# Attention scores as pairs of 64-row matmuls, with later transposes in the recurrence and a third plain MLP tile

## The chip, the core and the metric

The kernel runs on one core of a Trainium2 chip. Its engines work from queues of their own, each in order: TensorE (PE; loads of weights are shown apart as PEld), VectorE (DVE), ScalarE (ACT), GpSimd (POOL) and SyncE (SP), which here issues the DMAs. TensorE multiplies a moving operand (up to 512 columns) by weights that lie in its array of 128 rows and 128 columns, and writes to PSUM, eight banks of 512 f32 columns. The metric is the device time of one execution in microseconds.

## The reference

One layer of a diffusion backbone, batch 1, 1024 latent tokens with 256 context tokens ahead, width 1024, f32. What matters here:

```python
# inside each layer
aq, ak, av, bq, bk, bv, cq, cf, cb, ci, cg, gates = features(h_lat, w_in, ...)   # h @ w_in, split; rope, RMS of heads
yc = hgrn2_bidir(cq, cf, cb, ci, cg, ...)            # recurrence in both directions, 4 heads of 128
ya = window_attn(aq, ak, av, cak, cav, sink_a)       # 8 heads of 64, 2 kv heads; 256 context keys + band of 3 blocks + sink
yb = global_attn(bq, bk, bv, cbk, cbv)               # 8 heads of 64, 2 kv heads; 256 context + 1024 latent keys
x_mix = x + m_lat[2] * (sum_n sigmoid(gate_n) * (y_n @ w_branch[n])) @ w_out
u = dwconv(h2 @ w_up, w_dw, b_dw)                    # two halves a and g of 2816 channels, conv over 3 tokens
x = x_mix + m_lat[5] * ((a * silu(g)) @ w_down)
out = rms_norm(x, norm_final)
```

The scores are `q . k / 8`, in the attention of both kinds with 4 query heads per kv head; the softmax is over all keys that a query may see. In the recurrence the output of each head is RMS-normed over its 128 channels, scaled and multiplied by `silu(cg)`.

## The kernel before

f32 products are made from two parts. A value is split into a high part that TensorE's f32r format holds and the rest (`h` and `l`, written by an ACT copy and a DVE subtraction); a product of matrices is three f32r matmuls, high by high, high by low, low by high (L199 to L201, L841 to L843, L917 to L919).

The stages follow each other: modulation and context, the recurrence head by head (`hgrn_head`, L1040), token-major projections with rope, window attention, global attention, merging of the branches, output projection, the MLP's up products, its down products, the last norm.

**Attention.** Each of 16 iterations takes 128 queries and one kv head, so 4 query heads. `qprep` splits the queries and lays, for each head, 64 rows of high part and 64 rows of low part one above the other, so that QT[:, h] has 128 rows. The keys stand twice in KH and twice in KL, in rows 0 to 63 and again in rows 64 to 127. One matmul of QT[:, h] with KH gives (high + low) by high, one with KL (high + low) by low: two matmuls per head and group of keys give all four products of parts. `softmax_window` (L1351) makes the scores of one head in one two-bank PSUM tile (tag mm, two of them: L1364 and L1365 for the context, L1367 and L1368 for the band, L1369 adds the mask), and DVE takes the maximum, ACT the exponential with the sum. `softmax_global` (L1392) makes the context scores of four heads in one tile (L1402, L1403) and then, head by head, 1024 latent scores in a tile each (L1412, L1413). The probabilities are transposed (L1298), split (L1302 and L1303) and multiplied with the values (L1284, L1285). Products for the merge gates (L199 to L201, tile gz) serve as filler. `weave` interleaves the scores of the next iteration, the values of this one and the filler by step counts; the framework's scheduler then sets each engine's order from data dependencies, priorities and its own estimates of duration.

**Recurrence.** `hgrn_head` ends, for each half of the tokens, with 12 matmuls for the output tile o (L1164 to L1166), ACT's square (L1167), DVE's sum, POOL's power, DVE's scaling into yo (L1172), four transposes oT of yo (L1175), DVE's product with gain and gate (L1177) and a store. The next head's projections (zf, zb) follow in the program and may be drawn ahead by the scheduler.

**MLP, up.** Of 22 tiles of 128 channels in each half, tiles 0 and 1 are plain products (`plain`, L755). From tile 2 on a recursive scheme with seven block products instead of eight is used (`w_sums`, `up_first`, `up_rest`), which needs sums of the weights and of the blocks of the activations: T1, T2, T3 and T4, made by DVE and ACT after tile 1. T4 takes the place of the block named 12. `act_out` does the convolution and the gate, `act_store` the store. L867 is DVE's sum that frees half of a PSUM tile in `up_rest`.

Of the kernel before, what the change touches and what calls it, by code (L numbers as in the profile page):

```python
# [18 lines left out]
P = 128  # L19
# [48 lines left out]
NB = 1  # L68
# [23 lines left out]
def build(tc, ins, out, dbg=None):  # L92
    nc = tc.nc
    V, A, G, T, SP = nc.vector, nc.scalar, nc.gpsimd, nc.tensor, nc.sync
    with ExitStack() as top:
# [697 lines left out]
        act_out(1, za)  # L793

        blk["T4"] = blk["12"]
# [4 lines left out]
        P1[0] = Aligned(p1s.enter_context(tc.tile_pool(name="p1", bufs=1, side="right", reuse_waits="tile")))  # L800

# [238 lines left out]
def hgrn_head(nc, cp, h, proj, early, mm2, bank, ident, masks, lb, oml, st_ctx, gnc, mhalf, y_d):  # L1040
# [116 lines left out]
    for g in range(2):  # L1157
        yo = cp.tile([P, 4, P], F32, tag="yo", name=f"yo{h}{g}", bufs=2)
        ys = cp.tile([P, 512], F32, tag="ys", name=f"ys{h}{g}", bufs=2)
        pt = bank("b", f"o{h}{g}")  # L1160
# [6 lines left out]
        A.activation(yo, pt, AF.Square)  # L1167
        rs = cp.tile([P, 4], F32, tag="ors", name=f"ors{h}{g}", bufs=2)
        V.reduce_sum(out=rs, in_=yo, axis=AX.X)
        V.tensor_scalar(out=rs, in0=rs, scalar1=1.0 / P, scalar2=EPS, op0=ALU.mult, op1=ALU.add)  # L1170
        G.tensor_tensor(out=rs, in0=rs, in1=mhalf[:, :4], op=ALU.pow)
        V.tensor_tensor(out=yo, in0=pt, in1=rs[:, :, None].to_broadcast([P, 4, P]), op=ALU.mult)  # L1172
        pt2 = bank("b", f"oT{h}{g}")
        for c in range(4):
            T.transpose(pt2[:, c], yo[:, c], ident)  # L1175
        sl = slice(g * 512, g * 512 + 512)
        V.scalar_tensor_tensor(out=ys, in0=pt2.rearrange("p a b -> p (a b)"), scalar=gnc, in1=cg[:, sl],  # L1177
                               op0=ALU.mult, op1=ALU.mult)
        SP.dma_start(y_d[2, h][:, sl], ys)
# [26 lines left out]
def attention(tc, nc, ap_, br, ins, kv_d, q_d, y_d, mm2, bank, ident, identr, fill_gen, fill_steps):  # L1206
# [45 lines left out]
    def qprep(it):  # L1252
# [4 lines left out]
        qs = tl([P, 4, 2, 64], "qs", f"q{it}", dt=F32R)  # L1257
        A.activation(qs[:, :, 0], qf, AF.Copy, scale=QSCALE)
        V.scalar_tensor_tensor(out=qs[:, :, 1], in0=qf, scalar=QSCALE, in1=qs[:, :, 0].bitcast(F32),
                               op0=ALU.mult, op1=ALU.subtract)  # L1260
# [79 lines left out]
    for it in range(n_it):  # L1340
# [4 lines left out]
        weave((scores(it + 1), S_LEN * (4 + br)) if it + 1 < n_it else (None, 0),  # L1345
              (values(it, PT, kts), len(kts) + 1),
              (some(fill_gen, b - a), b - a))
    man.close()


def softmax_window(nc, tl, mm2, tt, g, nm, QT, KH, KL, trir, identr, snk, nsnk, res):  # L1351
# [9 lines left out]
    for h in range(4):  # L1361

        sc = mm2(f"sa{nm}{h}").rearrange("p a b -> p (a b)")[:, 256:256 + nk]
        T.matmul(sc[:, :256], QT[:, h], KH[:, g, :256], start=True, stop=False)  # L1364
        T.matmul(sc[:, :256], QT[:, h], KL[:, g, :256], start=False, stop=True)  # L1365
        k = (2 + lo) * P
        T.matmul(sc[:, 256:], QT[:, h], KH[:, g, k:k + w], start=True, stop=False)  # L1367
        T.matmul(sc[:, 256:], QT[:, h], KL[:, g, k:k + w], start=False, stop=False)  # L1368
        T.matmul(sc[:, 256:], identr, trir[:, m0:m0 + w], start=False, stop=True)  # L1369
        n1 = ng[:, h:h + 1]  # L1370
        hs = g * 4 + h
        V.tensor_reduce(out=n1, in_=sc, axis=AX.X, op=ALU.max, negate=True)

        V.tensor_tensor(out=n1, in0=n1, in1=nsnk[:, hs:hs + 1], op=ALU.min)
        pw = tl([P, 640], "pw", f"{nm}{h}", 8)
        A.activation(pw[:, :nk], sc, AF.Exp, bias=n1, accum_out=sm[:, h:h + 1])
        Ps.append(pw)
        if h % NB == NB - 1:
            b = slice(h - NB + 1, h + 1)
            bs = slice(hs - NB + 1, hs + 1)  # L1380
# [4 lines left out]
            for j in range(h - NB + 1, h + 1):  # L1385
                G.tensor_scalar(out=Ps[j][:, :nk], in0=Ps[j][:, :nk], scalar1=sm[:, j:j + 1], scalar2=1.0,
                                op0=ALU.mult, op1=ALU.mult)
# [4 lines left out]
def softmax_global(nc, tl, mm2, g, nm, QT, KH, KL, res, rs):  # L1392
# [5 lines left out]
    nc_, ng, sm, r = st[:, 0], st[:, 1], st[:, 2:4], st[:, 4]  # L1398
    pc = tl([P, 4, 256], "pc", nm)
    sc = mm2(f"sbc{nm}").rearrange("p a (b c) -> p (a b) c", b=2)  # L1400
    for h in range(4):
        T.matmul(sc[:, h], QT[:, h], KH[:, g, :256], start=True, stop=False)  # L1402
        T.matmul(sc[:, h], QT[:, h], KL[:, g, :256], start=False, stop=True)  # L1403
# [4 lines left out]
    for h in range(4):  # L1408
        s2 = mm2(f"sbl{nm}{h}")
        for hf in range(2):  # L1410
            k = 256 + hf * 512
# [142 lines left out]
```

## Time and profile before

| | |
|---|---|
| median of 3 runs | 2142.07 us (2141.16 to 2144.56) |
| the profiled execution's own time | 2145.39 us |
| its span | 2143.6 us |
| TensorE busy | 2089.5 us, 97% of the span |
| DVE, ACT, POOL busy | 1391.7, 1005.2, 301.0 us |
| recurrence, heads 0 to 3 | about 159 to 445 us |
| window attention scores | from 708.1 us to 885.9 us |
| global attention | from about 918 us to 1228 us |
| recursive up tiles | from about 1490 us to 1881 us |

A row of the groups or of the timeline names a line, an engine, the operation, what it writes and reads, the array's rows and columns used (128\*64: 128 rows, 64 columns), the shape, and the time. In the timeline the first number is the start and the second how long the instruction or the merged group took; a matmul's end is modelled, and neighbours overlap, so the distance between starts says how long one holds the engine. A bracket is idle time before the instruction, with the one that ended it. In the busy times by stage the columns are the stretch, its length, the busy time and count of PE, PEld, DVE, ACT and POOL, the granted PE clock, and two of DMA.

### The profile page before, as it was taken

How to read it: one execution, taken by the hardware profiler on the slowest of the kernel's cores; microseconds unless marked ns; L12 is line 12 of the kernel's file. 1: busy time of each engine (PE TensorE's matmuls, PEld its weight loads, DVE VectorE, ACT ScalarE, POOL GpSimd, SP SyncE). 2: the span in 40 equal slices, each digit the busy share in tenths (PEclk: the TensorE clock that was granted, in tenths of full speed). 3: DMA queues.
4: the chain of work that ended last, by engine and by line, in shares of the span. 5: the costliest groups of instructions: out<-in, count | busy, mean ns of one | idle time of the engine just before them, and what ended most of it. 6: DMA issues, size and time to landing. Idle time of an engine off the chain costs nothing. (4 is left out here: it accounts for less than half of the span.)

```text
span 2143.6 us, 30557 instructions
## 1 busy us (share of the span) xinstructions
PE 2089.5 (97%) x11674; PEld 1741.4 (81%) x11674; DVE 1391.7 (65%) x2306; ACT 1005.2 (47%) x1768; POOL 301.0 (14%) x262
## 2 busy tenths in 40 slices
PE   7999999999999999999999999999999999999997
PEld 4887887888988888878888788887788888888887
DVE  4736746626565687678887746569777777664433
ACT  3333322411122777688888734346445444453322
POOL 0001000010022222100000000011533444200111
PEclk9999999999999999999999999999999999999999
DMA  9511111126644221211100354541222222285342
GB/s 352 210 43 41 39 41 40 50 97 206 198 136 130 77 60 41 73 66 35 35 28 28 115 197 145 191 158 40 98 89 80 78 89 79 89 289 193 107 127 89
DMA packets 95492, 229.29 MB, mean 107 GB/s; under 512 B 10737, under 2 KB 35825, under 8 KB 94321
## 3 DMA queue, kind: packets, MB, share of 16 engines
q1 hardware_dynamic: 95344, 227.33, 32.0%
q8 instruction: 92, 1.51, 0.3%
q14 instruction: 56, 0.45, 0.1%
HBM read 181.68 MB, written 45.61 MB: 106 GB/s over the span
## 5 line engine op out<-in xcount | busy, mean ns | idle before, releaser
L175 ACT CAST wh<-wr 128x1024 fp32r<-128x1024 f32 x137 | 143.3, 1046 | 401.2 <-PE dn L918 73.2
L176 DVE TENSOR_TENSOR wl<-wr,wh 128x1024 fp32r<-128x1024 f32 x137 | 168.9, 1233 | 240.6 <-ACT wh L175 227.2
L1303 DVE TENSOR_TENSOR pl<-pp,ph 128x512 fp32r<-128x512 f32 x236 | 159.5, 688 | 29.1 <-ACT ph L1302 23.3
L199 PE MATMUL gz<-hh,wh 128*128 128x512 f32 x384 | 156.2, 407 | 3.6 <-ACT gs L523 3.5
L1302 ACT CAST ph<-pp 128x512 fp32r<-128x512 f32 x236 | 135.7, 587 | 37.5 <-PE pp L1298 35.4
L201 PE MATMUL gz<-hh,wl 128*128 128x512 f32 x384 | 152.2, 397 | 0.0
L200 PE MATMUL gz<-hl,wh 128*128 128x512 f32 x384 | 152.2, 396 | 0.0
L210 PE MATMUL tm<-wl,hh 128*128 128x256 f32 x384 | 108.9, 283 | 3.1 <-DVE wl L176 3.1
L209 PE MATMUL tm<-wh,hh 128*128 128x256 f32 x384 | 108.8, 283 | 0.7 <-ACT qo L613 0.7
L211 PE MATMUL tm<-wh,hl 128*128 128x256 f32 x384 | 108.6, 283 | 0.0
L1284 PE MATMUL po<-ph,VHL 128*128 128x512 f32 x236 | 106.1, 450 | 1.5 <-ACT ph L1302 1.0
L918 PE MATMUL dn<-ac,wh 128*128 128x512 f32 x256 | 99.7, 390 | 0.0
L919 PE MATMUL dn<-ac,wl 128*128 128x512 f32 x256 | 99.6, 389 | 0.0
L917 PE MATMUL dn<-ac,wh 128*128 128x512 f32 x256 | 99.6, 390 | 0.0
L1285 PE MATMUL po<-pl,VHL 128*128 128x512 f32 x236 | 97.0, 411 | 0.1
L199 PEld LDWEIGHTS gz<-hh,wh 128*128 128x128 f32 x384 | 72.8, 189 | 17.7 <-ACT gs L523 5.7
L201 PEld LDWEIGHTS gz<-hh,wl 128*128 128x128 f32 x384 | 72.5, 189 | 14.9
L200 PEld LDWEIGHTS gz<-hl,wh 128*128 128x128 f32 x384 | 72.8, 190 | 11.6
L731 ACT ACTIVATE u<-c,cw 128x1024 f32<-128x1024 f32 x40 | 50.0, 1249 | 66.3 <-DVE c L878 35.5
L210 PEld LDWEIGHTS tm<-wl,hh 128*128 128x128 f32 x384 | 73.7, 192 | 4.1 <-DVE wl L176 3.7
L1298 PE MATMUL pp<-ident,plat 128*128 128x128 f32 x512 | 76.7, 273 | 0.0
L1298 PEld LDWEIGHTS pp<-ident,plat 128*128 128x128 f32 x512 | 62.8, 140 | 16.9 <-DVE pl L1303 1.2
(1448 smaller groups left out, 5958.8 us busy)
## 6 DMA issues: line engine op xcount, KB each, us to landing
wr<-in_w_cm SPq DMA_DIRECT2D x48, 512.0 KB, 3.6
wr<-in_w_up SPq DMA_DIRECT2D x44, 512.0 KB, 3.5
wr<-in_w_down SPq DMA_DIRECT2D x33, 512.0 KB, 3.5
wmr<-in_w_mod SPq DMA_DIRECT2D x32, 512.0 KB, 4.6
gate_d<-gs SPq DMA_DIRECT2D x48, 256.0 KB, 2.4
sgt<-gate_d SPq DMA_DIRECT2D x24, 512.0 KB, 3.4
act_d<-u SPq DMA_DIRECT2D x22, 512.0 KB, 2.6
st<-act_d SPq DMA_DIRECT2D x44, 256.0 KB, 3.8
```

The lines of the kernel that those rows point to most:

```text
L175: A.copy(hi[:, :n], raw[:, :n])
L176: (lo_eng or V).tensor_tensor(out=lo[:, :n], in0=raw[:, :n], in1=hi[:, :n].bitcast(F32), op=ALU.subtract)
L199: T.matmul(psl, wh[:, k, c], hh[:, k0 + k, cols], start=s, stop=False)
L200: T.matmul(psl, wh[:, k, c], hl[:, k0 + k, cols], start=False, stop=False)
L201: T.matmul(psl, wl[:, k, c], hh[:, k0 + k, cols], start=False, stop=e)
L209: T.matmul(psl, hh[:, k, toks], wh[:, k % 4, :], start=s, stop=False)
L210: T.matmul(psl, hh[:, k, toks], wl[:, k % 4, :], start=False, stop=False)
L211: T.matmul(psl, hl[:, k, toks], wh[:, k % 4, :], start=False, stop=e)
L1284: T.matmul(po, vv, ph, start=n == 0, stop=False)
L1298: T.transpose(pp[:, h], PT(h, n), ident)
L1302: A.copy(ph, pp)
L1303: V.tensor_tensor(out=pl, in0=pp, in1=ph.bitcast(F32), op=ALU.subtract)
```

## The change

Three edits.

*Scores.* `qprep` now lays the high parts of two heads one above the other, and their low parts likewise, so that rows 0 to 63 hold one head and rows 64 to 127 another. Each score group is made by `pair_scores`: three products (high by high, low by high, high by low; low by low is left out) for the two heads in turn, each a matmul over 64 rows of the array, head 2a in rows 0 to 63 and head 2a + 1 in rows 64 to 127, in different PSUM tiles. A pair takes both tiles of tag mm. The context scores in the global stage lie in another order of heads. QT has two buffers instead of three, and the step counts of `weave` change (2 + br in place of 4 + br).

*Recurrence.* The norm up to yo stays where it was, and the transposes with what follows them become a function (`turn`) that the next head calls behind its two forget gates; for the last head the gate products that follow call them.

*MLP.* Tile 2 of the up products is a plain one; its second-half products of the first four blocks stand ahead of T4's split, the rest behind it.

```diff
-            for h in range(CH):
-                hgrn_head(nc, c1, h, proj, early, mm2, bank, ident, masks, lb, oml, st_ctx, gnc, mhalf, y_d)
+            late = []
+            for h in range(CH):
+                late = hgrn_head(nc, c1, h, proj, early, mm2, bank, ident, masks, lb, oml, st_ctx, gnc, mhalf, y_d, late)
             for n, i in gates[:4]:
-                for _ in gate_unit(c1, n, i, "mm"):
-                    pass
+                for j, _ in enumerate(gate_unit(c1, n, i, "mm")):
+                    if late and j % 8 == 7:
+                        late.pop(0)()
...
+        ws = up_units(2)
+        za = [mm2(f"up2{s}") for s in (1, 0)][::-1]
+
+        for s in (1, 0):
+            plain([za[s][:, 1]], [ws[s]], 1, range(KQ))
         blk["T4"] = blk["12"]
...
+        for s in (1, 0):
+            plain([za[s][:, 1]], [ws[s]], 1, range(KQ, KT))
+            plain([za[s][:, 0]], [ws[s]], 0, range(KT))
+        act_store()
+        act_out(2, [[z.rearrange("p a b -> p (a b)")] for z in za])
...
-        for f in range(2, FT):
+        for f in range(3, FT):
...
         forget(nc, cp, z, F1[:, d], KS[:, d], lb[:, d * 4 + h:d * 4 + h + 1], oml[:, d * 4 + h:d * 4 + h + 1],
                L, f"{nm}{h}")
+        if late:
+            late.pop(0)()
...
+        def turn():
+            pt2 = bank("b", f"oT{h}{g}")
+            for c in range(4):
+                T.transpose(pt2[:, c], yo[:, c], ident)
...
+        return turn
...
-        for h in range(4):
-            T.transpose(pq[:, h], qs[:, h].rearrange("p a b -> p (a b)"), identr)
-        QT = tl([P, 4, P], "QT", it, 3, F32R)
+        for part in range(2):
+            for a in range(2):
+                T.transpose(pq[:, 2 * part + a], qs[:, part, 2 * a:2 * a + 2].rearrange("p a b -> p (a b)"), identr)
+        QT = tl([P, 4, P], "QT", it, 2, F32R)
...
-        weave((scores(it + 1), S_LEN * (4 + br)) if it + 1 < n_it else (None, 0),
+        weave((scores(it + 1), S_LEN * (2 + br)) if it + 1 < n_it else (None, 0),
...
+def pair_scores(T, zs, a, QT, KH, KL, g, k, n, more=False):
+
+    for j, (part, K) in enumerate(((0, KH), (1, KH), (0, KL))):
+        for r, z in enumerate(zs):
+            rows = slice(r * 64, r * 64 + 64)
+            T.matmul(z, QT[rows, 2 * part + a], K[rows, g, k:k + n], start=j == 0, stop=j == 2 and not more)
...
-        T.matmul(sc[:, :256], QT[:, h], KH[:, g, :256], start=True, stop=False)
-        T.matmul(sc[:, :256], QT[:, h], KL[:, g, :256], start=False, stop=True)
...
+        scs = [mm2(f"sa{nm}{2 * a + r}").rearrange("p a b -> p (a b)")[:, 256:256 + nk] for r in range(2)]
+        pair_scores(T, [sc[:, :256] for sc in scs], a, QT, KH, KL, g, 0, 256)
+        pair_scores(T, [sc[:, 256:] for sc in scs], a, QT, KH, KL, g, (2 + lo) * P, w, True)
...
-    for h in range(4):
-        s2 = mm2(f"sbl{nm}{h}")
+    for a in range(2):
+        s2 = [mm2(f"sbl{nm}{2 * a + r}") for r in range(2)]
         for hf in range(2):
-            k = 256 + hf * 512
-            T.matmul(s2[:, hf], QT[:, h], KH[:, g, k:k + 512], start=True, stop=False)
-            T.matmul(s2[:, hf], QT[:, h], KL[:, g, k:k + 512], start=False, stop=True)
+            pair_scores(T, [s_[:, hf] for s_ in s2], a, QT, KH, KL, g, 256 + hf * 512, 512)
```

How the order of the instructions moves is seen at three places of TensorE's queue. First the global stage, the third and fourth head of iteration 4 (tiles sbl_2 and sbl_3). Before, the two matmuls of each 512 keys stand together, one head at a time:

```order
4441 L200 MATMUL gz_9659<-hl,wh_9655 128x512
4442 L201 MATMUL gz_9659<-hh,wl_9656 128x512
4443 L1412 MATMUL sbl_2_9736<-KH_0_8659,QT_4_9414 128x512
4444 L1413 MATMUL sbl_2_9736<-KL_0_8660,QT_4_9414 128x512
4445 L1412 MATMUL sbl_2_9736<-KH_0_8659,QT_4_9414 128x512
4446 L1413 MATMUL sbl_2_9736<-KL_0_8660,QT_4_9414 128x512
4447 L1298 MATMUL pp_9746<-ident,plat_3_0_9458 128x128
```

Now (x2 stands for two such matmuls in a row):

```order
4556 L1321 MATMUL pp_9959<-ident,plat_3_3_9719 128x128
4557 L1379 MATMUL sbl_2_9931<-KH_0_8787,QT_4_9578 128x512 x2
4558 L1379 MATMUL sbl_2_9931<-KL_0_8788,QT_4_9578 128x512
4559 L1379 MATMUL sbl_2_9931<-KH_0_8787,QT_4_9578 128x512 x2
4560 L1379 MATMUL sbl_2_9931<-KL_0_8788,QT_4_9578 128x512
4561 L1307 MATMUL po_9823<-ph_34_9911,VHL_0_8789 128x512
4562 L1379 MATMUL sbl_3_9932<-KH_0_8787,QT_4_9578 128x512 x2
4563 L1379 MATMUL sbl_3_9932<-KL_0_8788,QT_4_9578 128x512
4564 L1379 MATMUL sbl_3_9932<-KH_0_8787,QT_4_9578 128x512 x2
4565 L1379 MATMUL sbl_3_9932<-KL_0_8788,QT_4_9578 128x512
```

The two heads were written in turn, matmul by matmul; in the queue all six of the one head stand ahead of all six of the other.

Second the window stage, the first heads of iteration 6 (tiles sa_0 and sa_1). Before, one head's five matmuls:

```order
3282 L1364 MATMUL sa_0_7072<-KH_0_5968,QT_6_6914 128x256
3283 L1365 MATMUL sa_0_7072<-KL_0_5969,QT_6_6914 128x256
3284 L1367 MATMUL sa_0_7072<-KH_0_5968,QT_6_6914 128x384
3285 L1368 MATMUL sa_0_7072<-KL_0_5969,QT_6_6914 128x384
3286 L1369 MATMUL sa_0_7072<-trir_0_5973,identr 128x384
```

Now:

```order
3312 L1286 MATMUL pq_7112<-identr,qs_q_7109 128x128
3313 L1379 MATMUL sa_0_7120<-KH_0_5968,QT_6_6954 128x256
3314 L1379 MATMUL sa_1_7121<-KH_0_5968,QT_6_6954 128x256
3315 L1379 MATMUL sa_0_7120<-KH_0_5968,QT_6_6954 128x256
3316 L1379 MATMUL sa_1_7121<-KH_0_5968,QT_6_6954 128x256
3317 L1379 MATMUL sa_0_7120<-KL_0_5969,QT_6_6954 128x256
3318 L1379 MATMUL sa_1_7121<-KL_0_5969,QT_6_6954 128x256
```

Here the heads alternate in the queue as they do in the program.

Third the recurrence, the outputs o and transposes oT of head 0. Before, the transposes of the first half stand ahead of the outputs of the second:

```order
414 L201 MATMUL zf_1515<-hh,wl_1512 128x512
...
416 L200 MATMUL zf_1515<-hl,wh_1511 128x512
417 L1175 MATMUL oT_1413<-ident,yo_1392 128x128 x4
418 L1164 MATMUL o_1422<-Vt_1046,S_1117 128x128
419 L1165 MATMUL o_1422<-ST_1331,QQ_986 128x128
```

Now:

```order
416 L1198 MATMUL o_1413<-ST_1331,QQ_986 128x128
417 L1199 MATMUL o_1413<-ST_1331,QQ_986 128x128
418 L198 MATMUL zf_1501<-hh,wh_1497 128x512
...
429 L200 MATMUL zf_1501<-hh,wl_1498 128x512
430 L1183 MATMUL oT_1555<-ident,yo_1405 128x128 x4
431 L198 MATMUL zb_1568<-hh,wh_1564 128x512
```

The outputs of both halves come first, then twelve products of the next head's zf, then the first transposes.

More of the change, by code (lines that the diff above doesn't have):

```diff
@@ L1037, in head_rms, with hgrn_head @@
     return r
[L1040 removed]
+def hgrn_head(nc, cp, h, proj, early, mm2, bank, ident, masks, lb, oml, st_ctx, gnc, mhalf, y_d, late):
     V, A, G, T, SP = nc.vector, nc.scalar, nc.gpsimd, nc.tensor, nc.sync
@@ L1166, in hgrn_head @@
             T.matmul(o, QQ[:, 0, sl], ST[:, 1, c], start=False, stop=True)
[L1167 to L1179, printed above, removed]
+        late.append(norm(g, pt))
+    return late
 def some(gen, n):
@@ L1384, in softmax_window @@
             V.reciprocal(sm[:, b], sm[:, b])
-            for j in range(h - NB + 1, h + 1):
-                G.tensor_scalar(out=Ps[j][:, :nk], in0=Ps[j][:, :nk], scalar1=sm[:, j:j + 1], scalar2=1.0,
-                                op0=ALU.mult, op1=ALU.mult)
+            G.tensor_scalar(out=pw[:, :nk], in0=pw[:, :nk], scalar1=sm[:, b], scalar2=1.0, op0=ALU.mult, op1=ALU.mult)
         yield
@@ L1397, in softmax_global @@
     st = tl([P, 5, 4], "st", nm)
-    nc_, ng, sm, r = st[:, 0], st[:, 1], st[:, 2:4], st[:, 4]
+    nc_, ng, sm = st[:, 0], st[:, 1], st[:, 2:4]
     pc = tl([P, 4, 256], "pc", nm)
[L1400 to L1403, printed above, removed]
+    sc = mm2(f"sbc{nm}").rearrange("p r (a c) -> p r a c", a=2)
+    for a in range(2):
+        pair_scores(T, [sc[:, r, a] for r in range(2)], a, QT, KH, KL, g, 0, 256)
+    sc = sc.rearrange("p r a c -> p (r a) c")
     V.tensor_reduce(out=nc_, in_=sc, axis=AX.X, op=ALU.max, negate=True)
```

73 lines of the change are left out of this document (42 added, 31 removed).

## The prediction

> **What bounds the kernel now.** I read the page first, then the busy time by stage, then the waits of TensorE, then single starts in its timeline. The page says that TensorE (PE) has work nearly all the time; the two attention stages, where the scores are made, say it more sharply:
>
> ```profile
> span 2143.6 us, 30557 instructions
> PE 2089.5 (97%) x11674; PEld 1741.4 (81%) x11674; DVE 1391.7 (65%) x2306; ACT 1005.2 (47%) x1768; POOL 301.0 (14%) x262
> ...
> 720.00:890.00 170.00, 169.11 (x1009) 145.85 (x1008) 134.82 (x414) 124.28 (x320) 47.44 (x61) 1.00 0.16 50
> 935.00:1210.00 275.00, 273.47 (x1587) 224.76 (x1586) 222.48 (x373) 226.40 (x487) 6.04 (x15) 1.00 0.10 32
> ```
>
> In the window stage (720 to 890 us) PE is busy 99%, in the global stage (935 to 1210) 99%, at the full granted clock, while DVE and ACT stand at 80% and 82%. The score matmuls hardly wait for another engine: this group has the most, 1.3 us in 128 matmuls, for what ACT had still to read from a scores buffer.
>
> ```profile
> L1412 PE MATMUL sbl<-KH,QT 128*128 128x512 f32 x128 | 51.8, 405 | 1.3 <-ACT pc__8872 L1405 1.3
> ```
>
> So attention takes as long as its matmuls take to issue one behind another. "Busy" does not price that, since neighbours overlap; the distance between starts does.
>
> ```profile
> 1502.06 0.39 PE L842 MATMUL upd<-T1l,ws2h 128*128 128x512 f32 x1
> 1502.29 0.39 PE L843 MATMUL upd<-T1h,ws2l 128*128 128x512 f32 x1
> 1502.52 0.39 PE L841 MATMUL upd<-T1h,ws2h 128*128 128x512 f32 x1
> ...
> 2117.82 0.33 PE L917 MATMUL dl<-ac,wh 128*128 128x384 f32 x1
> 2118.86 0.33 PE L917 MATMUL dl<-ac,wh 128*128 128x384 f32 x1
> ...
> 1076.25 0.60 PE L1298 MATMUL pp<-ident,plat 128*128 128x128 f32 x4
> 1076.61 0.47 PE L1284 MATMUL po<-ph,VHL 128*128 128x512 f32 x1
> 1076.92 0.39 PE L1285 MATMUL po<-pl,VHL 128*128 128x512 f32 x1
> 1077.18 0.50 PE L1284 MATMUL po<-ph,VHL 128*128 128x512 f32 x1
> 1077.52 0.28 PE L1402 MATMUL sbc__10700<-KH,QT 128*128 128x256 f32 x1
> 1077.63 0.28 PE L1403 MATMUL sbc__10700<-KL,QT 128*128 128x256 f32 x1
> 1077.75 0.28 PE L1402 MATMUL sbc__10700<-KH,QT 128*128 128x256 f32 x1
> ...
> 2127.10 0.28 PE L917 MATMUL dl<-ac,wh 128*128 128x128 f32 x1
> 2127.21 0.28 PE L918 MATMUL dl<-ac,wh 128*128 128x128 f32 x1
> ```
>
> A slot of 512 columns costs 0.227 us, one of 384 costs 0.174 (2117.82 to 2118.86 in six steps), one of 256 costs 0.12. The 128-column pair stops at 0.11, above a quarter of 0.227: a load of 128 columns of weights takes that long, and is hidden under every wider matmul. After a transpose (1076.61 to 1076.92) the first plain matmul holds PE 0.31, 0.086 more.
>
> **The scores, slot by slot.** Before: per head two matmuls over all 128 rows. The loops give 288 slots of 256 columns (160 window, 128 global), 96 of 384 and 256 of 512: 288 x 0.12 + 96 x 0.174 + 256 x 0.227 = 109.4 us. After: 432, 144 and 384 matmuls of 64 rows each, half as many again, which pay only where one on rows 0-63 and one on rows 64-127 run at once, so where they are neighbours in PE's order. The trace has no 64-row matmul. It has pairs side by side in 64 columns each, the recurrence's scores:
>
> ```profile
> 168.06 0.39 PE L201 MATMUL zq<-hh,wl 128*128 128x512 f32 x1
> 168.28 0.39 PE L199 MATMUL zq<-hh,wh 128*128 128x512 f32 x1
> 168.60 1.15 PE L1106 MATMUL sc<-QQ,KC 128*64 128x64 f32 x32
> 169.68 0.50 PE L200 MATMUL zq<-hl,wh 128*128 128x512 f32 x1
> 170.02 0.39 PE L201 MATMUL zq<-hh,wl 128*128 128x512 f32 x1
> 170.25 0.40 PE L199 MATMUL zq<-hh,wh 128*128 128x512 f32 x1
> ...
> L1106 PE MATMUL sc<-QQ,KC x768: 222/222/272, 159.9 to 420.1; 128*64 128x64 f32 x192
> ...
> 200.63 0.39 PE L1164 MATMUL o<-Vt,S 128*128 128x128 f32 x2
> 200.85 0.39 PE L1165 MATMUL o<-ST,QQ 128*128 128x128 f32 x2
> ```
>
> An f32 matmul is recorded as two passes. The 32 passes of L1106 start within 1.15 - 0.22 = 0.93 us, 0.030 each. An undivided f32 pass over 128 columns takes 0.11 (two in 0.22, L1164 to L1165), so one over 64 would take 0.055: the pairs do overlap, and their weight loads with them. I take the same for rows.
>
> But the order decides what overlaps. In the global stage the second pair of heads stands as six matmuls of head 2, one value product, six of head 3: both need an emptied buffer, and the scheduler started each when its own was free. All six are on one half of the rows. Counted over PE's whole order, a matmul sharing a slot only with a neighbour on the other half, the changed kernel needs 260 slots of 256, 84 of 384 and 315 of 512: 31.2 + 14.6 + 71.5 = 117.3 us. That is **7.9 us more** than before; the window stage wins 3.1 of it (35.9 to 32.8), the global stage loses 11 (73.5 to 84.5).
>
> **The switch between shapes.** The same rows price it. L199 at 168.28 holds PE 0.32 before the divided array may start, 0.09 over its slot. Behind it (last pass starts 1.15 - 0.22 after 168.60, at 169.53) the next whole-array matmul starts 0.15 later where 0.05 would do: 0.10. Then L200 holds PE 0.34, 0.11 over its slot: its successor's weights could not be loaded ahead. Is that a matter of columns alone? A 2-row transpose, rows divided and columns whole, shows the way out too:
>
> ```profile
> 39.71 0.28 PE L305 MATMUL pm<-ident,row 2*128 2x2 f32 x2 [0.30 <-ACT row L349]
> 39.92 3.72 PE L432 MATMUL czf<-ch,wr 128*128 128x256 f32 x16
> 43.48 2.75 PE L432 MATMUL czb<-ch,wh 128*128 128x256 f32 x12
> ```
>
> The twelve take 2.75 - 0.38 = 11 x 0.216; the sixteen behind the switch take 3.34, 0.10 more than 15 x 0.216. So rows cost the same. The Trainium skill says this too: TensorEngine Tiling (Array Packing), section Key Properties, has it that changing the tiling mode, not just the tile, drains the engine. It speaks against this change: by it the free switch below falls away for 64 rows too, where the rows above, none of them with 64 rows, leave it open.
>
> In the changed order the 64-row matmuls stand in 150 stretches (38 window, 112 global), cut by transposes, value products and gate products. Way in: 0.09 plus one exposed load of 0.11, 0.20 each: 30 us. Way out: 89 times to a plain matmul, 0.10 + 0.11; 61 times to a transpose, whose load is half as long, 0.10 + 0.055: 28 us. In return 41 of the 313 transpose-to-matmul steps go, at 0.086: -3.5. Switches: **+54.5 us**. Bounds: nothing, if rows switch free; and, if the loads of the two halves do not overlap, 0.11 more on each way in (16), 0.10 on each of the 172 shared 256-slots (17) and 0.05 on the 60 shared 384-slots (3), so +36. I take 54.5, since its parts come from the nearest shapes.
>
> A pair now holds both scores buffers. The order puts some 26 PE rows, about 5 us, between a pair and the next, and a slower PE leaves ACT and DVE more time: 0, at most 0.3 us for each of 32 pairs (10 us).
>
> **The later transposes.** PE stands before the output transposes of each head:
>
> ```profile
> L1175 PE MATMUL oT<-ident,yo 128*128 128x128 f32 x32 | 5.2, 284 | 7.1 <-DVE yo L1172 7.1
> ...
> 200.14 0.66 PE L1175 MATMUL oT<-ident,yo 128*128 128x128 f32 x4 [0.98 <-DVE yo L1172]
> ```
>
> Eight waits, 7.1 us. In the new order twelve products of the next head, 12 x 0.227 = 2.7 us, stand behind the second half's outputs and ahead of the first transposes, so that wait goes in three heads. The last head has no next one: its transposes follow directly and keep their two waits. Gain 7.1 x 6/8 = **5.3 us** (0 to 7.1).
>
> **The third plain tile.** 96 matmuls instead of 84: 12 x 0.227 = 2.7 us more. It takes PE past a place where DVE is behind with the split blocks:
>
> ```profile
> 1498.08 0.50 PE L843 MATMUL upc<-T3h,vlS 128*128 128x512 f32 x1 [0.33 <-DVE vlS L680]
> ...
> 1505.47 0.50 PE L841 MATMUL up<-T2h,ws2h 128*128 128x512 f32 x1 [2.12 <-DVE c L867]
> ...
> 1527.71 0.66 PE L841 MATMUL up<-T2h,ws3h 128*128 128x512 f32 x1 [2.90 <-DVE c L867]
> 1528.17 0.63 PE L842 MATMUL up<-T2l,ws3h 128*128 128x512 f32 x1
> 1528.60 0.63 PE L843 MATMUL up<-T2h,ws3l 128*128 128x512 f32 x1
> ...
> 1528.00:1532.00 4.00, 4.00 (x12) 3.09 (x12) 1.00 (x1) 0.00 (x0) 3.92 (x4) 0.59 0.03 6
> ```
>
> Three waits, 5.35 us, and behind the longest the granted clock falls to 0.59: eight matmuls at 0.427 instead of 0.227, 1.6 us. With 96 x 0.227 = 21.8 us of products that need little of DVE, it catches up. Net 2.7 - 5.35 - 1.6 = **-4.3 us** (up to +2.7 if the waits only move on to the next tile's sum, L867).
>
> **Sum.** 7.9 + 54.5 - 5.3 - 4.3 = +52.8 us, on the profiled execution's 2145.4: 2198. That execution stood 3.3 over the median of 2142.1, so 2195.
>
> **Rivals.** *The switch is free for rows* (not slower): one mechanism, PE keeping its queue filled across shapes, at the 300 borders of the stretches. 7.9, plus 1.7 for 20 more transpose-to-matmul steps, minus 9.6: 0, so 2142. It decides from a border cost of nothing; each 0.01 us puts 3 us on it. For it: a 64-row tile keeps all 128 columns. Against it: the 2-row rows. Faster by much would take neighbours everywhere, 109.4 x 3/4 (27 less, 2105), which the order rules out.
> *Half price*: only the drains, or only the loads: 2168.
> *Weight loads do not hide*: the two halves load in turn, +36, 2231. Or a load on one's own rows waits for the running matmul: 277 neighbours on one half x 0.11 = 30, 2225; against it, whole-array matmuls hide theirs at 0.227. The Trainium skill, TensorE: Matmul & The Clock Gate, section The mechanism, has the second rule (a load overlaps a running matmul only on other row groups).
> *No overlap at all* of 64-row pairs: 164.1 us of slots instead of 117.3, +47, 2242. Against it: the paired columns.
>
> **Chances.** Forecast 0.66, half price 0.10, loads 0.08, free switch 0.10, no overlap 0.06. The forecast's own spread (the buffers, the two gains) is about 2180 to 2210. From 2155 to 2232 holds all but the free switch, no overlap and some tail. A measurement here cannot tell less than 0.2% (4.3 us). Faster 0.06 and same 0.05 are the free switch, slower 0.89 the rest.
>
> **What would show it.** Starts of two score matmuls on different halves a few ns apart, six of one half 0.227 apart; the matmul ahead of a stretch holding PE about 0.32, the one behind it 0.34; the attention stages longer by some 10 us (window) and 50 (global), with PE still busy throughout; the waits before the oT transposes gone in three heads of four; no wait at L867's successor and no fall of the clock near 1528. Pairs 0.227 apart rather than together would mean no overlap; a border matmul at 0.23 would mean that the switch is free, and the forecast wrong by its largest term.

## The result and the profile after

The changed kernel takes 2197.54 us (median of 4 runs, 2195.27 to 2198.77), the kernel before, beside it, 2141.61 (2140.79 to 2144.56). The ratio is 1.0257, 95% interval 1.024 to 1.0275: slower by 56 us. The forecast was 2195 us, with a range of 2155 to 2232. The profiled execution took 2198.77 us.

The page of the changed kernel shows TensorE (PE) as busy as before, and longer; the last row is the group of the global stage's score matmuls, with 0.5 us of idle time:

```profile
span 2197.0 us, 31231 instructions
...
PE 2152.3 (98%) x12006; PEld 1745.0 (79%) x12006; DVE 1390.6 (63%) x2299; ACT 998.9 (45%) x1761; POOL 287.7 (13%) x257
...
L1379 PE MATMUL sbl<-KH,QT 64*128 64x512 f32 x256 | 75.8, 425 | 0.5 <-ACT pc__9000 L1433 0.3
```

Where the time went is read from the starts of the stages' first matmuls. The attention runs from the first score matmul (sa) to the last value product (po). In the answers by tile the numbers behind the count are the shortest, median and longest duration in ns, and then the first and last start. The kernel before:

```profile
L1364 PE MATMUL sa<-KH,QT x64: 274/281/385, 708.1 to 885.8; 128*128 128x256 f32 x64
...
L1285 PE MATMUL po<-pl,VHL x236: 387/393/498, 722.8 to 1227.9; 128*128 128x512 f32 x118
```

The changed kernel:

```profile
L1379 PE MATMUL sa<-KH,QT x256: 271/333/443, 701.2 to 894.7; 64*128 64x256 f32 x80, 64*128 64x384 f32 x48
...
L1308 PE MATMUL po<-pl,VHL x236: 387/470/507, 719.4 to 1287.4; 128*128 128x512 f32 x118
```

1227.9 - 708.1 = 519.8 us have become 1287.4 - 701.2 = 586.2: 66.4 us more. With the other stages, each from its first matmul to that of the next (us):

| stage | before | after | difference |
|---|---|---|---|
| recurrence (zq to tm) | 363.9 | 357.2 | -6.7 |
| projections (tm to kt) | 232.7 | 234.7 | +2.0 |
| window (sa to sbc) | 210.2 | 227.6 | +17.4 |
| global (sbc to the last po) | 309.6 | 358.6 | +49.0 |
| up products (up to dn) | 436.4 | 430.3 | -6.1 |
| down products to the end | 262.0 | 262.0 | 0 |

What is left, -2.2 us, lies almost wholly ahead of the recurrence (-1.9). The projections, which none of the edits touches, took 228.4 to 234.7 us in the profiles of this document: a few us between two totals can come from there alone, so an edit's effect is read from its own stage.

How it looks inside is seen in the timeline of TensorE in the global stage. First a place where pairs are neighbours:

```profile
1100.56 0.40 PE L200 MATMUL gz<-hh,wl 128*128 128x512 f32 x1
1100.89 0.49 PE L1379 MATMUL sbl<-KH,QT 64*128 64x512 f32 x2
1101.31 0.66 PE L1321 MATMUL pp<-ident,plat 128*128 128x128 f32 x4
1101.90 0.50 PE L1379 MATMUL sbl<-KH,QT 64*128 64x512 f32 x2
1102.24 0.40 PE L1379 MATMUL sbl<-KL,QT 64*128 64x512 f32 x2
1102.47 0.62 PE L1379 MATMUL sbl<-KH,QT 64*128 64x512 f32 x4
1102.93 0.40 PE L1379 MATMUL sbl<-KL,QT 64*128 64x512 f32 x2
1103.26 0.66 PE L1321 MATMUL pp<-ident,plat 128*128 128x128 f32 x4
...
1107.77 0.73 PE L1379 MATMUL sbl<-KH,QT 64*128 64x512 f32 x2
1108.33 0.39 PE L1379 MATMUL sbl<-KL,QT 64*128 64x512 f32 x1
1108.56 0.62 PE L1379 MATMUL sbl<-KH,QT 64*128 64x512 f32 x2
1109.03 0.39 PE L1379 MATMUL sbl<-KL,QT 64*128 64x512 f32 x1
1109.35 0.33 PE L1321 MATMUL pp<-ident,plat 128*128 128x128 f32 x1
```

A pair costs one slot: the pair at 1102.24 is followed by the next 0.23 later, and the two members start 3 ns apart (1102.237 and 1102.240 in the trace). The borders cost what was forecast: the gate product L200 ahead of the pair at 1100.89 holds PE 0.33 instead of 0.227, the pair itself 0.42, the first pair at 1101.90 0.34. And from 1107.77 on six matmuls of one head stand alone, 0.23 us each apart from the borders at both ends, as many slots as six whole-array matmuls.

### The profile page after: what moved, and what is told of

Read it like the earlier page. It is cut to its first block, busy times and chain, and to the rows that moved or that the text cites. A ratio compares the mean times of both kernels' runs of the same rounds, so it can differ in the third digit from the quotient of the medians.

```text
span 2197.0 us, 31231 instructions
## 1 busy us (share of the span) xinstructions
PE 2152.3 (98%) x12006; PEld 1745.0 (79%) x12006; DVE 1390.6 (63%) x2299; ACT 998.9 (45%) x1761; POOL 287.7 (13%) x257
## 4 chain that ended last, share of the span: by engine, by line
PE 56%; DVE 2%; ACT 1%; issue 0%; DMA 0%; POOL 0%; DVEq 0%; ACTq 0%
PE sbl L1379 4%; PE pp L1321 3%; PE dn L928 3%; PE dn L929 3%; PE dn L927 3%; PE up L851 2%; PE up L853 2%; PE up L852 2%; PE po L1308 2%; PE po L1307 2%; PE br L199 2%; PE br L200 2%; PE br L198 2%; PE upc L853 2%; PE upd L853 2%; PE upd L852 2%
## 5 line engine op out<-in xcount | busy, mean ns | idle before, releaser
L174 ACT CAST wh<-wr 128x1024 fp32r<-128x1024 f32 (+1 forms) x139 | 145.1, 1045 | 399.7 <-PE dn L928 72.9
L175 DVE TENSOR_TENSOR wl<-wr,wh 128x1024 fp32r<-128x1024 f32 (+1 forms) x139 | 171.6, 1235 | 226.4 <-ACT wh L174 214.5
L200 PE MATMUL gz<-hh,wl 128*128 128x512 f32 x384 | 152.3, 397 | 0.0
L1308 PE MATMUL po<-pl,VHL 128*128 128x512 f32 x236 | 104.4, 442 | 1.4
L200 PEld LDWEIGHTS gz<-hh,wl 128*128 128x128 f32 x384 | 73.0, 190 | 15.6 <-issue 0.7
L1321 PE MATMUL pp<-ident,plat 128*128 128x128 f32 x512 | 81.1, 278 | 0.6 <-DVE st__9356 L1445 0.2
L1379 PE MATMUL sbl<-KH,QT 64*128 64x512 f32 x256 | 75.8, 425 | 0.5 <-ACT pc__9000 L1433 0.3
```

The lines of the kernel that those rows point to most:

```text
L175: (lo_eng or V).tensor_tensor(out=lo[:, :n], in0=raw[:, :n], in1=hi[:, :n].bitcast(F32), op=ALU.subtract)
L200: T.matmul(psl, wl[:, k, c], hh[:, k0 + k, cols], start=False, stop=e)
L1321: T.transpose(pp[:, h], PT(h, n), ident)
L1379: T.matmul(z, QT[rows, 2 * part + a], K[rows, g, k:k + n], start=j == 0, stop=j == 2 and not more)
```

## The experiments

The theory is that of the prediction: each stretch of 64-row matmuls pays at both ends (some 58 us for 150 stretches), and in the order that the scheduler makes, pairs save less in slots than the third product adds. The rivals: borders are free and the loss is a wait or the order; pairs do not overlap; the loss comes from the other two edits. All ratios below are to the kernel before, run beside each.

**Without the pairs (no_pairs).** The scores as before, the two other edits as changed.

```diff
-        scs = [mm2(f"sa{nm}{2 * a + r}")... for r in range(2)]
-        pair_scores(T, [sc[:, :256] for sc in scs], a, QT, KH, KL, g, 0, 256)
+        T.matmul(sc[:, :256], QT[:, h], KH[:, g, :256], start=True, stop=False)
+        T.matmul(sc[:, :256], QT[:, h], KL[:, g, :256], start=False, stop=True)
...
-        weave((scores(it + 1), S_LEN * (2 + br)) ...
+        weave((scores(it + 1), S_LEN * (4 + br)) ...
```

> The change without its scores: each score as before over all 128 rows, the later transposes and the third plain tile kept. Theory (the scores cost some 65 us through the borders between tile shapes and through halves that stand alone; the two other edits are gains by themselves): the recurrence stays 6.7 us shorter and the first plain up tiles 6.1 us shorter than before, as in the changed kernel, the attention is as before: 2142 - 13 = 2129, at most 2134. Rival (the scores are worth something, and the other edits carry the loss or disturb the later order): 2180 or more. Rival (the two gains are only the changed kernel's, whose slower attention leaves slack elsewhere): 2142.

Measured: 2128.03 us (2126.71 to 2128.41), ratio 0.9936, interval 0.9924 to 0.9949. It is the shortest of the three kernels; the gain over the kernel before is 0.6%, clear of its interval. Its attention by tile:

```profile
L1388 PE MATMUL sa<-KH,QT x64: 274/281/384, 696.9 to 874.1; 128*128 128x256 f32 x64
...
L1309 PE MATMUL po<-pl,VHL x236: 387/393/498, 711.0 to 1215.7; 128*128 128x512 f32 x118
```

518.8 us, as before the change (519.8); recurrence 357.2 and up products 429.9, as after it. So the scores alone cost 2197.54 - 2128.03 = 69.5 us (67.4 between the attention of the two profiles), and the two other edits give 13.3.

**The last head's transposes (last_transposes).** no_pairs, with the transposes of the last head written a whole gate product apart:

```diff
-                    if late and j % 8 == 7:
+                    if late and j % 16 == 15:
```

> The kernel without pairs, and the two groups of transposes of the last head of the recurrence written behind the first and the second gate product in place of behind half a one each; in PE's order the second group moves 12 gate products back, the first stays. Theory: the wait of 0.94 us ahead of the second group goes, the 0.97 ahead of the first stays: 2128.0 - 0.9 = 2127, which a median can hardly tell; the wait's row does. Rival: the wait goes on to the gate products, no change.

Measured: 2125.48 us (2124.84 to 2129.03), ratio 0.9935 (0.9922 to 0.9949), which cannot be told from no_pairs, as forecast. Of the two waits before oT, together 1.6 us there, one of 0.8 is left.

**All rows (all_rows).** The same instructions in the same order, each score matmul over the whole array:

```diff
-            rows = slice(r * 64, r * 64 + 64)
-            T.matmul(z, QT[rows, 2 * part + a], K[rows, g, k:k + n], ...)
+            T.matmul(z, QT[:, 2 * part + a], K[:, g, k:k + n], ...)
```

> The changed kernel with the same instructions in the same order on every engine, but each of the 960 score matmuls takes all 128 rows in place of 64; it then computes the sum of two heads' scores, so its output is not the reference's. Theory: neighbours no longer overlap, 164.1 us of slots in place of 117.3 (+46.8); the 150 stretches have no borders any more (-58.1), and 61 transposes are followed by a whole-array matmul at 0.086 each (+5.2): 2197.5 - 6.1 = 2191. The matmul ahead of a score matmul holds PE 0.227 instead of 0.326, the first after the stretch 0.227 instead of 0.34, and the neighbours of two heads start 0.227 apart instead of 0.003. Rival (no border cost; the loss comes from waits for the scores' buffers and the order): +46.8, so 2244, with the matmul ahead of a stretch at 0.227 in both kernels. Rival (pairs do not overlap and borders are free): 2197, the same as the changed kernel, with starts 0.227 apart in both.

Measured: 2194.73 us (2192.83 to 2196.57), ratio 1.0249 (1.0235 to 1.0263). The total does not tell the theories apart, the rows do. The same place of the order as above:

```profile
1102.43 0.39 PE L200 MATMUL gz<-hh,wl 128*128 128x512 f32 x1
1102.66 0.63 PE L1378 MATMUL sbl<-KH,QT 128*128 128x512 f32 x2
1103.13 0.60 PE L1321 MATMUL pp<-ident,plat 128*128 128x128 f32 x4
1103.49 0.71 PE L1378 MATMUL sbl<-KH,QT 128*128 128x512 f32 x2
```

The gate product now holds PE 0.23 instead of 0.33, and the two matmuls behind it take 0.47, two slots, where the pair with its way out took 0.42. Added up from the starts over both attention stages (from the first kt on), the steps that begin with a score matmul grow from 148.8 to 174.6 us (the overlap is lost), and all other steps shrink from 451.7 to 421.8 (the borders' outer halves are gone): -4.2 in all. So the borders are not waits: they go when the shape goes, with order and dependencies unchanged. Both rivals fall: free borders would have given 2244, and without overlap the starts would have been as far apart in the changed kernel. My own sum does not fit as well. It had -6.1; a term in it, the 0.086 for a matmul behind transposes, is no cost (below), so I should have had -11.3, which is 2186. A 512 slot takes 0.231 here rather than 0.227 (1.5 us), and some 5 us I cannot place.

**Borders by themselves (borders).** No layer; a fixed order of TensorE alone, 24 rounds of each group, in a single execution. One round of some of the groups, shortened from the program:

```python
def s_full(a, b, j): full(a, j), full(a, j + 1)               # F: whole array, 512 columns
def s_pair(a, b, j): pair(b, j), pair(b, j + 1)               # P: rows 0-63 and 64-127, two pairs
def s_half(a, b, j): row(b, 0, j), row(b, 0, j + 1)           # H: rows 0-63 alone
def s_fp(a, b, j):   full(a, j), pair(b, j)                   # FP
def s_ffpp(a, b, j): full(a, j), full(a, j + 1), pair(b, j), pair(b, j + 1)
def s_tp(a, b, j):   turn(a, j), pair(b, j)                   # four transposes, a pair
```

> No layer at all: zeros are stored, and TensorE runs groups of 24 rounds each, in a fixed order with no waits, of f32r matmuls with 128 columns of weights. Theory, period of one round: two whole-array matmuls of 512 (F) 0.454; two pairs of 64-row halves (P) 0.454; two of one and the same half (H) 0.454; one whole and one pair (FP) 0.454 + 0.41 = 0.86; two and two (FFPP) 0.908 + 0.41 = 1.32; one whole and one half (FH) 0.86 as well; 256 columns: two whole 0.24, two pairs 0.24, one and one (FP256) 0.65; two pairs of 384 0.348; four transposes and a pair (TP) some 0.27 more than four transposes and a whole matmul (TF). Rival (a border is free between the shapes, the changed kernel's long steps come from its waits): FP 0.454, FP256 0.24. Rival (a border costs only one way or only once per change of weights): FP 0.66. Rival (a half's load waits for its own running matmul): H 0.67 rather than 0.454.

The timeline of that kernel (fa: whole-array and transposes, rb: row halves; rows of one kind are merged):

```profile
18.46 11.04 PE L42 MATMUL faF<-K,Q 128*128 128x512 f32 x48
29.43 11.19 PE L46 MATMUL rbP<-K,Q 64*128 64x512 f32 x96
40.47 11.04 PE L46 MATMUL rbH<-K,Q 64*128 64x512 f32 x48
51.43 0.49 PE L42 MATMUL faFP<-K,Q 128*128 128x512 f32 x1
51.86 0.50 PE L46 MATMUL rbFP<-K,Q 64*128 64x512 f32 x2
52.29 0.50 PE L42 MATMUL faFP<-K,Q 128*128 128x512 f32 x1
...
72.22 0.73 PE L42 MATMUL faFFPP<-K,Q 128*128 128x512 f32 x2
72.89 0.73 PE L46 MATMUL rbFFPP<-K,Q 64*128 64x512 f32 x4
73.55 0.73 PE L42 MATMUL faFFPP<-K,Q 128*128 128x512 f32 x2
...
159.54 0.66 PE L54 MATMUL faTP<-idn,xf 128*128 128x128 f32 x4
160.12 0.50 PE L46 MATMUL rbTP<-K,Q 64*128 64x512 f32 x2
160.55 0.66 PE L54 MATMUL faTP<-idn,xf 128*128 128x128 f32 x4
```

48 whole-array matmuls take 11 us; 96 on alternating halves take the same 11 us; 48 on one half take the same again. So pairs overlap wholly, and a half alone is worth a whole slot, with its next load hidden although it goes to the rows that are running. A round of FP takes 0.865 us (52.29 - 51.43 = 0.86) where two slots are 0.454: 0.41 for one border in and one out, and so does the longer round: 73.55 - 72.22 = 1.33 against 0.908, 0.42. There the single steps are 0.341, 0.322, 0.334, 0.323: the matmul ahead of each border holds 0.10 more, the first behind it 0.11 more, in both directions. With one half in place of the pair (FH) a round is 0.86 as well; a pair of 256 columns takes 0.120, one of 384 0.173. A round of four transposes with a pair is 1.01 us (160.55 - 159.54), with a whole matmul 0.670: 0.34 for the two borders there. The theory's numbers hold but for the last, which was expected at 0.27. That is 0.20 in and 0.155 out less the 0.086 of a matmul behind transposes; without this false term it is 0.355. (One whole and one pair of 256 columns take 0.63 a round at first, where 0.65 was expected; later the clock falls in that group, see the end.)

**More borders (mask_between).** In the window stage the masks move between context and band scores:

```diff
         pair_scores(T, [sc[:, :256] for sc in scs], a, QT, KH, KL, g, 0, 256)
+        for sc in scs:
+            T.matmul(sc[:, 256:], identr, trir[:, m0:m0 + w], start=True, stop=False)
         pair_scores(T, [sc[:, 256:] for sc in scs], a, QT, KH, KL, g, (2 + lo) * P, w, True)
-        for sc in scs:
-            T.matmul(sc[:, 256:], identr, trir[:, m0:m0 + w], start=False, stop=True)
```

(and start and stop of the band products accordingly)

> The changed kernel, but in the window stage the two mask matmuls of a pair of heads stand between the context scores and the band scores instead of behind both: the same matmuls, cut into 75 stretches instead of 38 in that stage. Theory: 187 stretches in all, ways in 187 x 0.20, ways out 107 to a plain matmul at 0.21 and 80 to a transpose at 0.15, together 72 in place of 58 us, slots 0.9 less: +13, so 2211, all of it in the window stage. Rival (borders cost nothing or are paid only at transposes): 2197. Rival (only the drains cost, loads are hidden behind the masks): +7, 2204.

Measured: 2203.83 us (2200.93 to 2204.42), ratio 1.0299 (1.0285 to 1.0313), 9 us over the changed kernel's ratio. The window stage takes 235.6 us instead of 227.6: +8.0 where 13 were expected. What is missing lies in the waits of that stage. The changed kernel (us in total, times, longest):

```profile
PE pp L1321 <- DVE pl L1326: 3.4, 7, 1.7
```

mask_between:

```profile
PE pp L1321 <- DVE pl L1326: 1.7, 1, 1.7
```

A step from start to start is late by what it exceeds the slot of its columns. Steps late by over 0.35 us add up to 8.0 us in the changed kernel's window stage and 3.4 here. So 8.0 + 4.6 + 0.9 (slots) = 13.5 us for 37 more stretches, 0.36 each. Free borders fall. The total is what the rival of drains alone had forecast (2204), but the rows of mask_between speak against it:

```profile
758.19 0.62 PE L1397 MATMUL sa<-trir,identr 128*128 128x384 f32 x2
758.74 0.61 PE L1379 MATMUL sa<-KH,QT 64*128 64x384 f32 x4
```

The two masks of 384 columns take 0.55 us where two slots are 0.348. Over that stage the first of the two holds 0.28, the second 0.27, and the first pair of 384 behind them 0.28 (medians, slot 0.174): the matmul behind a border pays as well as the one ahead of it.

**Both heads in one tile (joint_tiles).** In the global stage a scores tile holds the same 512 keys of two heads:

```diff
-        s2 = [mm2(f"sbl{nm}{2 * a + r}") for r in range(2)]
-        for hf in range(2):
-            pair_scores(T, [s_[:, hf] for s_ in s2], a, QT, KH, KL, g, 256 + hf * 512, 512)
+        s2 = [mm2(f"sbl{nm}{a}{hf}") for hf in range(2)]
...
+        for hf, s_ in enumerate(s2):
+            pair_scores(T, [s_[:, r] for r in range(2)], a, QT, KH, KL, g, 256 + hf * 512, 512)
+            V.tensor_reduce(out=mx[:, hf], in_=s_, axis=AX.X, op=ALU.max, negate=True)
...
```

> The changed kernel, but in the global stage a scores tile holds the same 512 keys of two heads in place of 1024 keys of one head, so that both members of a pair become ready by the same buffer; the exponentials are then four of 512 columns per pair of heads instead of two of 1024. In PE's order the latent pairs alternate: 202.7 slots of 512 columns instead of 314.9, 97.8 of 256 instead of 108.2 (-26.7 us), and 137 stretches instead of 150 (-5.3 with the steps beside them). Theory: 2197.5 - 32 = 2165, still slower than before; the global stage 32 us shorter than the changed kernel's. Rival (borders alone cost; pairs on different halves gain nothing): 2192. Rival (what costs is that a pair holds both buffers; here both are held until the maxima of both are known): 2197 or more, with idle time of PE ahead of the scores.

Measured: 2189.86 us (2187.39 to 2190.05), ratio 1.0226 (1.0211 to 1.0242): 8 us less than the changed kernel where 32 were expected. TensorE's waits in the global stage:

```profile
PE sbl L1379 <- ACT plat L1452: 6.1, 18, 0.4
PE pp L1321 <- ACT pc__12427 L1456: 3.0, 2, 2.9
PE pp L1321 <- ACT QT L1288: 2.7, 10, 0.4
PE pp L1321 <- DVE pl L1326: 2.0, 8, 0.3
```

The busy time of the 360 latent score matmuls in most of that stage fell from 111.6 to 84.5 us, by the 27 expected. But steps late by over 0.3 us add up to 29.2 us, against 5.7 in the changed kernel: 23.5 of the gain were given back. -27 - 5 + 23.5 = -8.5 agrees with the total, but in part by chance: in the profiles the global stage is only 4.2 us shorter (354.5 instead of 358.6), and the projections, which this edit does not touch, are 5.0 shorter. So another 4 us of the gain, or more, are missing from the stage and not placed: a late step that stands at a border counts the border too.

**Tiles freed earlier (joint_early).** joint_tiles, but each half of the keys takes its exponentials with its own maximum at once:

```diff
-        V.tensor_tensor(out=mx[:, 0], in0=mx[:, 0], in1=mx[:, 1], op=ALU.min)
...
+                V.tensor_tensor(out=mx[:, r:r + 1], in0=mx[:, r:r + 1], in1=nc_[:, c:c + 1], op=ALU.min)
+                A.activation(pls[r][:, hf * 512:hf * 512 + 512], s_[:, r], AF.Exp, bias=mx[:, r:r + 1], ...)
```

> joint_tiles, but each half of the keys takes its exponentials with its own maximum as soon as it has it, so that a scores tile comes free without the other half (the softmax then mixes two maxima, so the output is not the reference's; the work is the same). In PE's order 207.3 slots of 512 columns and 112.0 of 256 (93.3 us with the window's 32.8; joint_tiles 90.5, the changed kernel 117.3), in 165 stretches (joint_tiles 137, the changed kernel 150): 63 us of borders in place of 58. Theory (joint_tiles lost some 22 us to waits of PE, because both tiles are held until the maxima of both are known): 2197.5 - 24 + 5 = 2179 if PE waits as little as in the changed kernel; the waits of the score matmuls on the exponentials, 6.1 us in joint_tiles, are near nothing. Rival (the waits come from the additional instructions on DVE and ACT, or from the order of the values): they stay at 22, and the time is 2195 to 2205.

Measured: 2186.45 us (2185.67 to 2188.9), ratio 1.0211 (1.0194 to 1.0228): between the theory and its rival, and not clear of joint_tiles, whose interval overlaps. The waits of the score matmuls:

```profile
PE sbl L1379 <- ACT plat L1447: 2.7, 10, 0.5
```

2.7 us instead of 6.1, and late steps of 17.1 us instead of 29.2. That points to tiles held for the other half's maximum as about half of what joint_tiles gave back. It is not shown alone, since the order changed too: 28 more stretches (10 us) and 2.8 us more of slots take up the 12 us, and the global stage is 353.5 us instead of 354.5. Which instruction of DVE or ACT sets the waits that stay was not settled.

**TensorE in the order of the program (in_order, in_order_no_pairs).** One line, in the changed kernel and in no_pairs:

```diff
-MAN = (False, False)
+MAN = (True, True)
```

> The changed kernel with TensorE's order in both attention stages as the program writes it, not as the scheduler sets it: pairs always alternate (85.9 us of slots instead of 117.3) and stand in 85 stretches instead of 150 (41 out to a plain matmul, 44 to a transpose: 32.4 us of borders instead of 58). Theory: 2197.5 - 31 - 26 = 2140 plus whatever PE then waits, since nothing is drawn ahead any more; and some 9 us slower than the same order with whole-array scores (in_order_no_pairs), since 32.4 of borders are more than the 23.5 of slots that the pairs save. Rival (the scheduler's order is all that was wrong, pairs in order win): faster than in_order_no_pairs by 20 or more.

> The kernel without pairs (later transposes and third plain tile kept), with TensorE's order in both attention stages as the program writes it. It is what in_order has to be compared with. Theory: 2128 plus the waits of an order in which nothing is drawn ahead; about 9 below in_order. Rival: 20 or more above it.

Measured: 2269.21 us (2266.17 to 2270.87) with pairs, ratio 1.0606 (1.0592 to 1.062), and 2165.69 (2160.58 to 2168.21) without, ratio 1.0121 (1.0107 to 1.0134): 104 us apart, not 9. Busy times in 260 us of the global stage, with pairs:

```profile
990.00:1250.00 260.00, 210.39 (x1200) 148.79 (x1200) 147.94 (x254) 155.42 (x329) 4.02 (x10) 0.95 0.07 22
```

and without:

```profile
960.00:1220.00 260.00, 243.82 (x1379) 196.37 (x1378) 190.44 (x321) 196.68 (x421) 5.23 (x13) 1.00 0.09 28
```

With pairs TensorE stands still for 49.6 of 260 us, at a granted clock of 0.95; without, for 16.2, at 1.00. One of the largest waits with pairs is that of the latent score matmuls on the exponentials that empty their tiles; without pairs there is no such row:

```profile
PE sbl L1379 <- ACT plat L1447: 20.0, 30, 1.1
```

My comparison was wrong because I let the waits cancel. A pair takes both scores tiles and cannot begin before both are read; a single head needs only one. These 20.0 us are the direct part. The rest is mostly PE waiting for the split probabilities (pr, po and pp on ph and pl: 52.7 us, without pairs 18.2) at the lower clock; that it follows from the same cause is argued, not separated. The rival (pairs in order win) fell by far.

## Why the prediction was right

**The order and the slots: right.** 117.3 us of slots were counted, with 31.5 us of the borders inside the stretches (150 x 0.21): 148.8. The steps of all score matmuls in the changed kernel's trace add up to 148.8. Pairs overlap wholly (members mostly 3 to 4 ns apart) and halves alone take 0.23, as said. (The 80% and 82% given for DVE and ACT are those of the global stage; in the window stage the rows give 79% and 73%. Nothing hangs on it.)

**The switch: right, its credit wrong.** Borders of 0.10 for the drain and 0.11 for the load on each side came out of borders (0.41 to 0.42 a round) and of the changed kernel's rows, and all_rows takes them away with the shape. The columns' price did hold for rows. The Trainium skill, TensorEngine Tiling (Array Packing), section Key Properties, says that a change of tiling mode drains the engine; the traces agree, with 0.10 on the matmul ahead of each border. The credit of -3.5 for 41 fewer steps from a transpose to a whole matmul was wrong. The group of borders with four transposes and a whole matmul shows it:

```profile
152.16 0.60 PE L54 MATMUL faTF<-idn,xf 128*128 128x128 f32 x4
152.51 0.48 PE L42 MATMUL rbTF<-K,Q 128*128 128x512 f32 x1
152.82 0.60 PE L54 MATMUL faTF<-idn,xf 128*128 128x128 f32 x4
```

The matmul behind the four transposes holds 0.315, but the last transpose only 0.029 instead of 0.109, so such a step costs 0.008 and not 0.086. I had priced one side of it; the prediction's own rows have both (four transposes from 1076.25 to 1076.61, 0.36 us where 4 x 0.109 is 0.44).

Without the credit the scores sum to 7.9 + 58 = 65.9 us, and the attention grew by 66.4. That it comes so close is partly luck, as the stages show. I had said about 10 and 50, without the credit it would be 12 and 54, and it was 17.4 and 49.0. The window stage has more late steps than before the change (over 0.35 us: 8.0 instead of 3.2 us), among them the small waits on pl that went in mask_between; I had forecast none. The global stage stayed 5 us under its share: 1 us of that is fewer late steps (over 0.3 us: 5.7 instead of 6.8), the rest is open.

**Weight loads hide on the same half.** 48 matmuls on one half take what 48 whole ones take (11.0 us). The Trainium skill, TensorE: Matmul & The Clock Gate, section The mechanism, says that a load overlaps running matmuls only where the row groups differ, though it also speaks of a background weight buffer; on the first the measurement decides against it here, and the rival at 2225 falls. Its 4 ns between the starts of neighbours on different row groups agree with the 3 to 4 ns of most pairs here.

**The buffers at nothing: right in the time, not in the reason.** I argued that PE reaches the next pair late enough. What kept the waits away is, as I read the order, that the scheduler split the pairs: then the 11 us of slots that the global stage lost are the buffers' price, counted under another name. That reading of the scheduler is argued, not shown. Shown is that the waits come where the pairs are kept together: 23.5 us more of late steps in joint_tiles, and in in_order 20.0 us of score matmuls waiting for their tiles.

**The later transposes: right, 1.4 small.** -5.3 forecast, -6.7 measured. The waits are gone in three heads, as in the first row, of head 0; in the last they stay:

```profile
200.05 0.60 PE L1183 MATMUL oT<-ident,yo 128*128 128x128 f32 x4
...
428.86 0.65 PE L1183 MATMUL oT<-ident,yo 128*128 128x128 f32 x4 [0.81 <-DVE yo L1178]
...
433.05 0.63 PE L1183 MATMUL oT<-ident,yo 128*128 128x128 f32 x4 [0.78 <-DVE yo L1178]
```

The term was taken from the bracketed idle times (7.1 us before). From start to start the same eight waits cost 8.35 us, and 1.91 are left: 6.4.

**The third plain tile: right, 1.8 small.** -4.3 forecast, -6.1 measured. No wait behind L867 is left there, and the clock stays at 1.00 in the first recursive tiles:

```profile
1577.00:1625.00 48.00, 48.00 (x213) 39.76 (x212) 31.79 (x34) 23.39 (x31) 19.52 (x15) 1.00 0.23 82
```

Before, the same three waits cost 5.8 us from start to start rather than 5.35. A fourth wait went that I had not counted, of a plain product on the split weights (tile wl, L176): 0.7 us from start to start at 1470.7. Some 0.6 us are left unplaced.

**The sum.** +7.9 + 58 - 6.7 - 6.1 = +53.1 on the profiled 2145.4 gives 2198.5; the profiled execution took 2198.8. With the forecast's own terms the sum was 2198 as well: that is luck, since the two gains were too small by 3.2 us together and the credit of 3.5 was not there.

## What to carry to other kernels

Row-packed pairs pay by the length of the stretch they stand in: here a stretch of twelve matmuls of 512 columns replaces eight whole-array ones and saves two slots, 0.454 us, of which one way in and one way out take 0.41; the window's stretches save 0.29 and lose. Count the borders in the engine's order before counting the slots, and ask what buffer each member of a pair waits for: members with buffers of their own are either waited for together or drift apart. Price a wait by the distance between starts, on both sides of it, not by the idle time in brackets.

## What the runs showed of the hardware that was not expected

Between a transpose and a whole-array matmul there is next to no price: 0.029 + 0.315 stands where 0.109 + 0.227 would, 0.008 more. And the granted clock fell under the small kernel of borders, without a wait for any other engine, in the group of one whole matmul and one half:

```profile
104.00:110.00 6.00, 6.00 (x15) 2.61 (x13) 0.00 (x0) 0.00 (x0) 0.00 (x0) 0.86 0.01 3
111.00:134.00 23.00, 23.00 (x33) 9.15 (x32) 0.00 (x0) 0.00 (x0) 0.00 (x0) 0.50 0.00 0
```

At 0.50 a round of that group took 1.446 us instead of 0.862. It was seen once more in the group of one whole and one pair of 256 columns (0.50 from 195 to 209 us, 1.02 us a round), and not in the groups of 512 columns with pairs ahead of it (1.00 from 51 to 104 us). What sets it off was not tried; the attention stages of the changed kernel show 1.00.
